# Eighteen of layer 0's thirty-two later modulation pieces computed during the key and query projections

## The chip, the cores and the metric

The kernel runs on one core of a Trainium2 chip. The metric is the device time of one execution in microseconds (us). The engines are TensorE (PE, matmuls; PEld is its weight loading), VectorE (DVE), ScalarE (ACT), GpSimd (POOL) and SyncE (SP), which here only issues DMAs. Each engine works through its own list of instructions; semaphores join the lists.

## The reference

Two layers of a diffusion backbone over 1024 latent tokens and 256 context tokens, model width 1024, all in float32. What this case touches is the beginning of layer 0:

```
silu_c = silu(c); silu_cc = silu(c_ctx)
mod_l = silu_c @ mod_w[0] + mod_b[0];  mod_c = silu_cc @ mod_w[0] + mod_b[0]
sh1, sc1, g1, sh2, sc2, g2 = split(mod_l, 6)          # and the same six of mod_c
h = modulate(rms_norm(x, norm1_g[0]), sh1, sc1)       # latent; context alike
b_g, c_g, xv, q, k, v = split(h @ w_in)
q = rms_norm(q, q_g); k = rms_norm(k, k_g)            # per head of 64; latent ones rotated too
y_conv = b_g * dwconv3(c_g * xv)
o = differential attention(q, k, v)
x = x + g1 * (concat(y_conv, o) @ w_out)
x = x + g2 * conv_ffn(modulate(rms_norm(x, norm2_g[0]), sh2, sc2))
```

`sh1` and `sc1` are needed before anything else. The other four vectors, `g1`, `sh2`, `sc2`, `g2`, for latent and context, are first read after the output projection. They are 4096 rows of `mod_w[0]`, that is 32 pieces of 128, each multiplied with two vectors.

## The kernel before, in words

Every float32 matrix product is three products of split numbers (high and low part of each factor, line 219 to 221), and 24 matmuls of 512 columns make one output tile. A weight unit of 128x1024 is loaded by SP (`wr`, line 107), its high part is cast by ACT (`wh`, line 113), its low part subtracted by DVE (`wl`, line 115). There are two `wr` buffers and five of `wh` and `wl`.

Layer 0's front runs in these stages, and `ev_in` calls them in turn:

- the first modulation vectors and the norms (`mod_start`, `norm`);
- `ev_qkv`: three projections, v, k and q, each over ten tiles of 128 tokens: two context tiles, then eight latent ones. Here the tiles of the keys are called K1 to K10, those of the queries Q1 to Q10. For v a tile is only copied and stored. For k and q each tile goes through `qk_post`: ACT squares it (`qsq`, line 528), DVE sums by head (`ss`, 530) and scales (`vv`, 359), GpSimd raises it to the power -1/2 (`rr`, 361), DVE multiplies (`qn`, 533) and rotates in four operations (`m1`, `m2`, lines 427 to 433; a context tile has a single multiplication `qr`, 537). Then `to_rows` has PE transpose the tile (`tpq`, 545), ACT copy it (`to`, 548) and SP store it. The transposes of a tile are put off: they stand behind the gemm of the tile two places later (`late`).
- the gates: `weave` mixes three generators by their shares: `ev_gates` (36 steps; gemms `pc`, `px`, `pb` and the short convolution), `mod_rest0` (32 steps) and `att_ctx` (the context's attention, 30 steps).

`mod_rest0` makes the 32 pieces. A piece is one 512 KB load on SP into one of two `mbw` buffers (line 312) and two DVE instructions with an accumulator (`mbj`, line 298), one for the latent vector, one for the context's. When all are done it adds the bias and makes two scales.

The order in which an engine's instructions stand is not that of the calls alone: the recording layer moves instructions of one engine past each other while they wait for others, by its own estimate of when they will be ready. On the chip each engine then keeps that order.

Of the kernel before, what the change touches and what calls it, by code (L numbers as in the profile page):

```python
# [54 lines left out]


MODA, MODT, MODR = 128, 3, 5


MOD0 = "TVGVTVTGTVGTVTVT"  # L60
# [13 lines left out]
def drain(gen):  # L74
    for _ in gen:
        pass


def pace(gen, i, n, total):

    for _ in range((i + 1) * total // n - i * total // n):
        next(gen, None)


def weave(*gens):

    live = [[g, n, 0] for g, n in gens]
    while live:
        e = min(live, key=lambda e: (e[2] + 0.5) / e[1])
        if next(e[0], StopIteration) is StopIteration:  # L90
            live.remove(e)
        e[2] += 1
# [46 lines left out]
class Net:  # L139
# [305 lines left out]
    def ev_in(self):  # L445
        nc, tc, I = self.nc, self.tc, self.I
        with ExitStack() as s0:
            hp = s0.enter_context(tc.tile_pool(name="hp", bufs=16, reuse_waits="tile"))
            self.bgp = s0.enter_context(tc.tile_pool(name="bgp", bufs=1, reuse_waits="tile"))
            ps = s0.enter_context(tc.tile_pool(name="psA", bufs=2, space=PSUM, reuse_waits="tile"))  # L450
            alloc = lambda: hp.tile([P, 2, 512], F32R, tag="h", name="h")
            allocc = lambda: hp.tile([P, 2, CTX], F32R, tag="hc", name="hc", bufs=8)
            hs = {c: [] for c in range(3)}
            chunks = ((2, 256, 1), (0, 512, 0), (1, 512, 0))
            with tc.tile_pool(name="xp", bufs=4, reuse_waits="tile") as xp:
                tl, nm = {}, {}

                def load(c, T):
                    src = I["ctxT"] if c == 2 else I["xT"][c]
                    tl[c] = []  # L460
                    for q in range(4):
                        t = xp.tile([P, 2, 512], F32, tag="xr", name="xr", bufs=8)
                        nc.sync.dma_start(t[:, :, :T], src[:, q * 2:(q + 1) * 2, :])
                        tl[c].append(t)

                xtmp = Pool(xp, {"t2k": ("t2k", 6)})
                self.mod_start(hp, ps, lambda: load(2, 256))
                self.ws.ahead = 1
                self.ws.prefetch()
                for c, T, v in chunks:  # L470
                    if c != 2:
                        load(c, T)
                    nm[c] = self.norm(lambda k, c=c, T=T: tl[c][k // 2][:, k % 2, :T], T, self.gs[(0, 1, v)],
                                      lambda k, v=v: self.modA[:, k, v:v + 1], allocc if c == 2 else alloc,
                                      xtmp, ps, hs[c], True)
                    if c == 2:
                        next(nm[2])
                for c, n in ((0, 2), (1, 0), (1, 1)):
                    if n != c:
                        next(nm[c])  # L480
                    drain(nm[n])
                self.ws.ahead = 2
            self.bgw = s0.enter_context(tc.tile_pool(name="bgw", bufs=1, reuse_waits="tile"))
            with tc.tile_pool(name="qkp", bufs=1, reuse_waits="tile") as qp:
                self.ev_qkv(qp, ps, hs)
            with tc.tile_pool(name="gp", bufs=1, reuse_waits="tile") as gp:
                weave((self.ev_gates(gp, ps, hs), 36), (self.mod_rest0(), 32), (self.att_ctx(gp, ps), 30))

    def ev_qkv(self, qp, ps, hs):
        nc, I = self.nc, self.I  # L490
        cosF, sinS = self.rope_tabs(qp)
        qkg = qp.tile([P, 4, 64], F32, name="qkg")
        nc.scalar.dma_start(qkg, I["qkg"])

        nc.vector.tensor_scalar(qkg[:, 0:2, :], qkg[:, 0:2, :], 0.125, None, op0=ALU.mult)
        tabs = {}
        for n, i in (("q", 0), ("k", 2)):
            A = qp.tile([P, 8, 64], F32, name=f"A{n}")
            B = qp.tile([P, 8, 64], F32, name=f"B{n}")
            nc.vector.tensor_tensor(A, cosF, qkg[:, i:i + 1, :].broadcast_to([P, 8, 64]), op=ALU.mult)  # L500
            nc.vector.tensor_tensor(B, sinS, qkg[:, i + 1:i + 2, :].broadcast_to([P, 8, 64]), op=ALU.mult)
            tabs[n] = (A, B)
        tmp = Pool(qp, {"t2k": ("t2k", 7), "qr": ("qr", 4)})
        late = []
        for proj in ("v", "k", "q"):
            W = [self.ws.get() for _ in range(4)]
            for tt in (8, 9, 0, 1, 2, 3, 4, 5, 6, 7):
                c, o = (2, (tt - 8) * P) if tt >= 8 else (tt // 4, (tt % 4) * P)
                pt = ps.tile([P, 512], F32, tag="mm", name="pt", bufs=5)
                self.gemm_tok(pt, W, hs[c], o)  # L510
                if len(late) > 1 or (late and proj == "v"):
                    late.pop(0)()
                if proj == "v":
                    vt = tmp.tile([P, 512], F32, tag="t2k", name="vt")
                    nc.scalar.copy(vt, pt)
                    nc.sync.dma_start(self.vD[tt * P:(tt + 1) * P, :], vt)
                else:
                    qr = self.qk_post(pt, tabs[proj], qkg[:, 0 if proj == "q" else 2, :], tt, tmp)
                    dst = self.qT if proj == "q" else self.kT
                    late.append(lambda qr=qr, dst=dst, tt=tt: self.to_rows(qr, dst, tt, tmp, ps))  # L520
        while late:
            late.pop(0)()
# [1135 lines left out]
```

## Time and profile before

| | us |
|---|---|
| median of 3 runs (2699.24 to 2708.37) | 2703.9 |
| the profiled execution | 2705.93 |
| its span, first to last instruction | 2704.1 |
| PE busy in the span | 2564.4 (95%) |
| DVE busy | 1971.4 (73%) |
| ACT busy | 1164.4 (43%) |
| POOL busy | 425.7 (16%) |

In the trace the keys are projected from about 111 to 174 us, the queries to about 239 us, the gates to 428 us. Busy time is the union of an engine's instructions; matmuls overlap in the pipeline. A wait is the idle time of an engine just ahead of an instruction, put down to what released it.

### The profile page before, as it was taken

What the parts mean: (1) busy time and instruction counts of PE and PEld (TensorE: products, weight loads), DVE (VectorE), ACT (ScalarE), POOL (GpSimd) and SP (SyncE); (2) the same over time, 40 slices, a digit from 0 to 9 for tenths busy, and PEclk for the clock granted to TensorE, in tenths of its full rate; (3) what the DMA queues carried; (4) which work ended last, traced back from release to release, by engine and by line L of the source; (5) the groups of instructions that cost most, each with busy time, mean ns of one, the idle gap of its engine ahead of it and who ended that gap; (6) DMA issues with size and microseconds to landing.
All of it is one profiled execution on the core that took longest, in us unless ns stands there. A gap on an engine that the chain in (4) does not pass through costs nothing.

```text
span 2704.1 us, 34748 instructions
## 1 busy us (share of the span) xinstructions
PE 2564.4 (95%) x12666; PEld 2153.4 (80%) x12666; DVE 1971.4 (73%) x3010; ACT 1164.4 (43%) x1749; POOL 425.7 (16%) x434
## 2 busy tenths in 40 slices
PE   7999998999998898999999998999999999999999
PEld 6877787888898787788887887777678788888887
DVE  7467865999898578877776977626658866666895
ACT  5322223666666454444444444233235444434342
POOL 3222112544432013000000001012203100000000
PEclk9999998999999999999999999999999999999999
DMA  6234535433333542434348665577662322225874
GB/s 253 92 98 140 181 122 159 132 119 121 106 98 102 201 138 86 146 123 133 127 132 301 225 220 171 163 203 224 202 232 81 102 85 86 78 87 174 288 235 158
DMA packets 209548, 414.01 MB, mean 153 GB/s; under 512 B 20320, under 2 KB 89568, under 8 KB 208992
## 3 DMA queue, kind: packets, MB, share of 16 engines
q1 hardware_dynamic: 206352, 406.41, 45.7%
q10 hardware_dynamic: 3024, 5.38, 0.6%
q8 instruction: 99, 1.62, 0.2%
q14 instruction: 73, 0.60, 0.1%
HBM read 341.98 MB, written 69.73 MB: 152 GB/s over the span
## 4 chain that ended last, share of the span: by engine, by line
PE 51%; DVE 14%; issue 12%; DMA 7%; ACT 2%; POOL 2%; SPq 0%; ACTq 0%; DVEq 0%; POOLq 0%
PE PA L219 4%; PE PA L220 4%; PE PA L221 4%; PE pd L220 3%; PE pd L221 3%; PE pd L219 3%; PE PB L220 2%; PE PB L221 2%; PE PB L219 2%; PE po L220 2%; PE po L221 2%; PE po L219 2%; DVE wl L115 2%; DMA mw<-in_mod1T 1%; DMA r<-in_w_up 1%
## 5 line engine op out<-in xcount | busy, mean ns | idle before, releaser
L113 ACT CAST wh<-wr 128x1024 fp32r<-128x1024 f32 x254 | 262.0, 1033 | 411.5 <-PE PA L220 69.6
L115 DVE TENSOR_TENSOR wl<-wr,wh 128x1024 fp32r<-128x1024 f32 (+1 forms) x217 | 273.4, 1262 | 165.0 <-ACT wh L113 162.7
L219 PE MATMUL pd<-s,wh 128*128 128x512 f32 x616 | 240.8, 391 | 4.9 <-ACT s L967 4.9
L220 PE MATMUL pd<-s,wh 128*128 128x512 f32 x616 | 241.1, 391 | 2.0 <-DVE s L968 2.0
L221 PE MATMUL pd<-s,wl 128*128 128x512 f32 x616 | 240.6, 391 | 0.0
L219 PE MATMUL PA<-s,wh 128*128 128x512 f32 x544 | 212.1, 390 | 3.6 <-DVE a L897 3.6
L221 PE MATMUL PA<-s,wl 128*128 128x512 f32 x544 | 211.7, 389 | 0.0
L220 PE MATMUL PA<-s,wh 128*128 128x512 f32 x544 | 211.6, 389 | 0.0
L353 DVE SCALAR_TENSOR_TENSOR mw<-mw,cr 128x256 f32<-128x256 f32 x256 | 111.9, 459 | 82.6 <-DMA mw<-in_mod1T 73.6
L113 ACT CAST wh<-r 128x1024 fp32r<-128x1024 f32 x80 | 67.0, 837 | 219.2 <-PE PB L220 125.2
L361 POOL TENSOR_TENSOR rr<-vv,mhalf 128x8 f32<-128x8 f32 (+2 forms) x39 | 57.6, 1478 | 554.9 <-DVE vv L359 545.8
L219 PEld LDWEIGHTS pd<-s,wh 128*128 128x128 f32 x616 | 116.0, 188 | 29.7 <-ACT s L967 5.8
L220 PEld LDWEIGHTS pd<-s,wh 128*128 128x128 f32 x616 | 116.2, 189 | 27.7 <-DVE s L968 3.6
L221 PEld LDWEIGHTS pd<-s,wl 128*128 128x128 f32 x616 | 116.2, 189 | 24.2
L1480 ACT ACTIVATE p<-S,s 128x1280 f32<-128x1280 f32 (+1 forms) x80 | 92.8, 1160 | 81.3 <-DVE s L1478 73.0
L219 PE MATMUL PB<-s,wh 128*128 128x512 f32 x320 | 124.6, 389 | 1.2 <-ACT p L893 1.2
L220 PE MATMUL PB<-s,wh 128*128 128x512 f32 x320 | 124.5, 389 | 0.0
L221 PE MATMUL PB<-s,wl 128*128 128x512 f32 x320 | 124.5, 389 | 0.0
L219 PEld LDWEIGHTS PA<-s,wh 128*128 128x128 f32 x544 | 102.1, 188 | 26.5 <-DVE a L897 5.3
L822 POOL MEMSET a<- 128x1 f32 x44 | 4.3, 98 | 737.1 <-DVE fcv L707 734.4
L221 PEld LDWEIGHTS PA<-s,wl 128*128 128x128 f32 x544 | 102.1, 188 | 21.2
L220 PEld LDWEIGHTS PA<-s,wh 128*128 128x128 f32 x544 | 102.1, 188 | 21.0
(388 smaller groups left out, 7355.2 us busy)
## 6 DMA issues: line engine op xcount, KB each, us to landing
wr<-in_w_up SPq DMA_DIRECT2D x98, 512.0 KB, 3.4
wr<-in_w_dn SPq DMA_DIRECT2D x92, 512.0 KB, 4.2
gr<-gD SPq DMA_DIRECT2D x154, 256.0 KB, 4.1
mw<-in_mod1T SPq DMA_DIRECT2D x256, 128.0 KB, 3.3
gD<-fcv SPq DMA_DIRECT2D x44, 512.0 KB, 3.6
wr<-in_w_out SPq DMA_DIRECT2D x40, 512.0 KB, 4.2
r<-in_w_up SPq DMA_DIRECT2D x40, 512.0 KB, 3.3
mbw<-in_mod0T SPq DMA_DIRECT2D x32, 512.0 KB, 3.8
```

Source lines behind the costliest of these rows:

```text
L113: self.nc.scalar.copy(hi, raw)
L115: eng.tensor_tensor(lo, raw, hi.bitcast(F32), op=ALU.subtract)
L219: mm(out, L[0], R[0], start=first, stop=False)
L220: mm(out, L[0], R[1], start=False, stop=False)
L221: self.last_mm = mm(out, L[1], R[0], start=False, stop=last)
L353: self.nc.vector.scalar_tensor_tensor(w, in0=w, scalar=1.0, in1=c, op0=ALU.mult, op1=ALU.mult, accum_out=d)
L361: self.last_pow = nc.gpsimd.tensor_tensor(r, vv, self.mhalf[:, :n], op=ALU.pow)
L822: self.nc.gpsimd.memset(a[:, 0:1], 0.0)
L1480: nc.scalar.activation(e, sv, AF.Exp, bias=s2[:, m:m + 1], accum_out=self.s1[:, qt:qt + 1] if m == 0 else s2[:, 2:3])
```

## The change

`mod_rest0` is created ahead of `ev_qkv` and handed to it. From the eleventh tile on, that is for the twenty tiles of k and q, `ev_qkv` takes pieces from the generator behind each tile's gemm, 16 over the 20 tiles. The `weave` of the gates goes on with the same generator at 16 steps in place of 32.

```
+MOD1 = 16
...
             with tc.tile_pool(name="qkp", bufs=1, reuse_waits="tile") as qp:
-                self.ev_qkv(qp, ps, hs)
+                mod = self.mod_rest0()
+                self.ev_qkv(qp, ps, hs, mod)
             with tc.tile_pool(name="gp", bufs=1, reuse_waits="tile") as gp:
-                weave((self.ev_gates(gp, ps, hs), 36), (self.mod_rest0(), 32), (self.att_ctx(gp, ps), 30))
+                weave((self.ev_gates(gp, ps, hs), 36), (mod, 32 - MOD1), (self.att_ctx(gp, ps), 30))
...
-        late = []
+        late, n = [], 0
...
                 self.gemm_tok(pt, W, hs[c], o)
+                n += 1
+                if n > 10:
+                    pace(mod, n - 11, 20, MOD1)
                 if len(late) > 1 or (late and proj == "v"):
```

`pace(gen, i, n, total)` takes the i-th share of `total` steps over n calls. Lines behind the diff's places are three to seven higher in the kernel after (`mbj` is line 301, `qn` 540).

On DVE, the first latent tiles of the keys. Before, tile K3 and the start of K4 (the names are those of the program, `Ak` and `Bk` the rotation tables):

```order
L530 TENSOR_REDUCE ss<-qsq 128x8
L359 TENSOR_SCALAR vv<-ss 128x8
L533 TENSOR_TENSOR qn<-pt,rr 128x512
L427 TENSOR_TENSOR m_1031<-qn,Ak 128x512
L431 TENSOR_TENSOR m_1033<-qn,Bk 128x16x16 x2
L433 TENSOR_TENSOR m_1031<-m_1031,m_1033 128x512
L530 TENSOR_REDUCE ss<-qsq 128x8
```

After, the same tile:

```order
L537 TENSOR_REDUCE ss<-qsq 128x8
L301 SCALAR_TENSOR_TENSOR mbj,modB<-mbw,crow 128x1024
L362 TENSOR_SCALAR vv<-ss 128x8
L301 SCALAR_TENSOR_TENSOR mbj,modB<-mbw,crow 128x1024
L540 TENSOR_TENSOR qn<-pt,rr 128x512
L301 SCALAR_TENSOR_TENSOR mbj,modB<-mbw,crow 128x1024
L430 TENSOR_TENSOR m_1043<-qn,Ak 128x512
L434 TENSOR_TENSOR m_1045<-qn,Bk 128x16x16 x2
L301 SCALAR_TENSOR_TENSOR mbj,modB<-mbw,crow 128x1024
L436 TENSOR_TENSOR m_1043<-m_1043,m_1045 128x512
L537 TENSOR_REDUCE ss<-qsq 128x8
```

Four `mbj` stand inside K3's chain, one of them between `vv` and `qn`, where GpSimd works. By tile there are now 3 (K1), 3 (K2), 4 (K3), 4 (K4) and 2 (K5), 16 in all; before there were none.

On DVE, a latent tile of the queries. Before, tile Q4 (`Aq`, `Bq` are the queries' tables):

```order
L530 TENSOR_REDUCE ss<-qsq 128x8
L359 TENSOR_SCALAR vv<-ss 128x8
L533 TENSOR_TENSOR qn<-pt,rr 128x512
L427 TENSOR_TENSOR m_1586<-qn,Aq 128x512
L431 TENSOR_TENSOR m_1588<-qn,Bq 128x16x16 x2
L433 TENSOR_TENSOR m_1586<-m_1586,m_1588 128x512
```

After, the same tile:

```order
L537 TENSOR_REDUCE ss<-qsq 128x8
L301 SCALAR_TENSOR_TENSOR mbj,modB<-mbw,crow 128x1024
L362 TENSOR_SCALAR vv<-ss 128x8
L301 SCALAR_TENSOR_TENSOR mbj,modB<-mbw,crow 128x1024
L540 TENSOR_TENSOR qn<-pt,rr 128x512
L301 SCALAR_TENSOR_TENSOR mbj,modB<-mbw,crow 128x1024
L430 TENSOR_TENSOR m_1652<-qn,Aq 128x512
L434 TENSOR_TENSOR m_1654<-qn,Bq 128x16x16 x2
L301 SCALAR_TENSOR_TENSOR mbj,modB<-mbw,crow 128x1024
L436 TENSOR_TENSOR m_1652<-m_1652,m_1654 128x512
```

By tile of the queries there are now 3 (Q1), 4 (Q2), 3 (Q3), 4 (Q4), 4 (Q5) and 2 (Q6), 20 in all; before there were six, in Q1 to Q3, one of them between `vv` and `qn`. So 36 of the 64 `mbj`, 18 pieces, stand in the two projections, and 28 in the gates (58 before).

## Rows read from the trace of the kernel before

**Rows 1.** Windows: stretch, length, busy us (x instructions) by engine, granted clock, DMA.
```profile
111.00:174.00 63.00, 62.84 (x293) 51.66 (x291) 35.07 (x64) 15.64 (x24) 15.24 (x10) 1.00 0.26 80
174.00:239.00 65.00, 59.12 (x279) 48.85 (x280) 43.42 (x80) 14.03 (x23) 16.75 (x10) 0.97 0.31 99
239.00:378.00 139.00, 131.28 (x693) 109.92 (x692) 123.01 (x234) 36.77 (x80) 19.87 (x32) 0.99 0.58 188
378.00:428.00 50.00, 49.89 (x263) 42.28 (x261) 12.97 (x24) 8.78 (x16) 3.30 (x6) 1.00 0.24 79
```
**Rows 2.** Waits of DVE, 111 to 239 us: total us, times, longest.
```profile
DVE qn L533 <- POOL rr L361: 33.9, 19, 1.8
DVE ss L530 <- ACT qsq L528: 6.0, 9, 2.3
DVE mbj L298 <- DMA mbw<-in_mod0T: 2.3, 1, 2.3
```
**Rows 3.** DVE's timeline, tiles K2, K3, K6, K7: start, us, instruction [idle before].
```profile
123.17 0.69 DVE L530 TENSOR_REDUCE ss<-qsq 128x8 f32<-128x512 f32 x1 [0.55 <-ACT qsq L528]
129.53 0.69 DVE L530 TENSOR_REDUCE ss<-qsq 128x8 f32<-128x512 f32 x1 [2.30 <-ACT qsq L528]
...
147.27 0.69 DVE L530 TENSOR_REDUCE ss<-qsq 128x8 f32<-128x512 f32 x1 [0.38 <-ACT qsq L528]
148.00 0.17 DVE L359 TENSOR_SCALAR vv<-ss 128x8 f32<-128x8 f32 x1
149.98 0.69 DVE L533 TENSOR_TENSOR qn<-pt,rr 128x512 f32<-128x512 f32 x1 [1.81 <-POOL rr L361]
...
153.19 0.69 DVE L530 TENSOR_REDUCE ss<-qsq 128x8 f32<-128x512 f32 x1 [0.32 <-ACT qsq L528]
```
**Rows 4.** The same view, tiles Q1 to Q5.
```profile
180.90 0.69 DVE L530 TENSOR_REDUCE ss<-qsq 128x8 f32<-128x512 f32 x1 [0.90 <-ACT qsq L528]
...
189.05 1.22 DVE L298 SCALAR_TENSOR_TENSOR mbj<-mbw,crow 128x1024 f32<-128x1024 f32 x1
190.19 0.17 DVE L359 TENSOR_SCALAR vv<-ss 128x8 f32<-128x8 f32 x1
190.31 1.22 DVE L298 SCALAR_TENSOR_TENSOR mbj<-mbw,crow 128x1024 f32<-128x1024 f32 x1
193.06 0.69 DVE L533 TENSOR_TENSOR qn<-pt,rr 128x512 f32<-128x512 f32 x1 [1.52 <-POOL rr L361]
...
203.09 0.68 DVE L530 TENSOR_REDUCE ss<-qsq 128x8 f32<-128x512 f32 x1
...
208.59 0.68 DVE L530 TENSOR_REDUCE ss<-qsq 128x8 f32<-128x512 f32 x1
```
**Rows 5.** GpSimd's timeline: the power of K6 and of Q2.
```profile
148.31 1.64 POOL L361 TENSOR_TENSOR rr<-vv,mhalf 128x8 f32<-128x8 f32 x1 [4.34 <-DVE vv L359]
190.51 2.53 POOL L361 TENSOR_TENSOR rr<-vv,mhalf 128x8 f32<-128x8 f32 x1 [6.93 <-DVE vv L359]
```
**Rows 6.** PE's timeline: the transposes of K6 and of Q3.
```profile
157.30 0.60 PE L545 MATMUL tpq<-ident,m 128*128 128x128 f32 x4
203.58 0.60 PE L545 MATMUL tpq<-ident,m 128*128 128x128 f32 x4
```
**Rows 7.** Waits of PE, 174 to 239 us.
```profile
PE tpq L545 <- DVE m L433: 3.3, 1, 3.3
PE pt L220 <- DVE wl L115: 2.5, 1, 2.5
```
**Rows 8.** Waits of PE, 239 to 378 us (the two largest of six).
```profile
PE tpp L1510 <- DVE p L1493: 2.4, 5, 1.0
PE orb L377 <- POOL r L1533: 1.6, 1, 1.6
```
**Rows 9.** Tile mbw: its loads, and who waited for them.
```profile
  DVE mbj L298: 11.2, 8
...
DMA to landing us min/median/max: 3.2/3.8/7.4
```

More of the change, by code (lines that the diff above doesn't have):

```diff
@@ L484, in ev_in, with ev_qkv @@
             with tc.tile_pool(name="qkp", bufs=1, reuse_waits="tile") as qp:
-                self.ev_qkv(qp, ps, hs)
+                mod = self.mod_rest0()
+                self.ev_qkv(qp, ps, hs, mod)
             with tc.tile_pool(name="gp", bufs=1, reuse_waits="tile") as gp:
-                weave((self.ev_gates(gp, ps, hs), 36), (self.mod_rest0(), 32), (self.att_ctx(gp, ps), 30))
-    def ev_qkv(self, qp, ps, hs):
+                weave((self.ev_gates(gp, ps, hs), 36), (mod, 32 - MOD1), (self.att_ctx(gp, ps), 30))
+    def ev_qkv(self, qp, ps, hs, mod):
         nc, I = self.nc, self.I
```

## The prediction

> **What bounds the kernel now.** I read the busy time by stage first [rows 1]. While the keys are projected (111 to 174 us) PE is busy for 62.8 of 63 us and DVE for 35.1. While the queries are (174 to 239 us) PE is busy for 59.1 of 65, DVE for 43.4. In the first part of the gates (239 to 378 us) DVE is busy for 123.0 of 139 us and PE leaves 139 - 131.3 = 7.7 us idle; in the rest PE is busy throughout. So PE sets the pace nearly everywhere, and where it stops in the gates it is mostly DVE that is late: five waits for `p`, which DVE combines, and one for `r`, a power that hangs on DVE's `e` [rows 8]. By shares, DVE has 27.9 us free beside the keys and 21.6 us beside the queries.
>
> The next view is what DVE waits for in those two stages, since free time counts only if a moved instruction fits into it. Of the idle time 33.9 us are 19 waits of `qn` for GpSimd's power, 6.0 us are 9 waits of `ss` for ACT's square [rows 2]. DVE's list is in order, and the chain of one tile is serial: `ss`, `vv`, power, `qn`, rotation. In K6 `ss` starts at 147.27 and the next one at 153.19, of which only 0.32 us is a wait for the new tile; 1.81 us is the wait for the power in the middle [rows 3]. So DVE's chain for one tile takes 5.6 us of the 5.9 us that PE needs for one, although DVE is idle for more than a third of it.
>
> The third view is how much delay PE tolerates. K6's last rotation is over at about 152.9 us (the next `ss` starts after a 0.32 us wait at 153.19), and PE transposes K6 at 157.30 [rows 3, 6]: 4.4 us of slack. In the queries it is nearly gone: Q3's chain ends when the next `ss` starts, at 203.09, and its transpose is at 203.58 [rows 4, 6]. From there DVE starts each `ss` right behind the last rotation, 5.50 us apart (203.09 to 208.59) with no wait in front. The six `mbj` that already stand in Q1 to Q3 have done that. At the end of the queries PE stops for 3.3 us for a rotated tile, at their beginning for 2.5 us for a `wl` [rows 7]: at both ends DVE's queue decides.
>
> **What the change removes.** Thirty of the 58 `mbj` leave the gates. At 1.22 us each [rows 4] this is 36.6 us of DVE's 123.0 us there, so its share falls from 88% to 62%. The gain is bounded by PE's idle time, 7.7 us [rows 1], and by zero, since the matmuls stay. Not all of it can go: `p` and `qa` also wait for loads, ACT and GpSimd, and a stall that goes leaves the next of these last. I take 4.5 us, a little over half, because the waits named in rows 8 alone are 4.0 us and hang on DVE.
>
> **What it adds in the keys.** First the price of one `mbj` inside a chain. From its start at 189.05 to `vv` at 190.19 it holds the queue for 1.14 us, call it 1.15; between two `mbj` the accumulator's read makes it 1.26. Between `vv` and `qn` one would expect it to be free, for there DVE waits 1.8 us anyway. The trace shows it once, in Q2: `vv` at 190.19, `mbj`, `qn` at 193.06, which is 2.87 us, where K6 without one has 148.00 to 149.98, 1.98 us. The power itself took 2.53 us in place of 1.64 [rows 3 to 5]. So there it costs 0.89 us.
>
> The Trainium skill explains why (SBUF — State Buffer, Who interferes with whom): a DVE instruction with two inputs in SBUF takes its second through the read interface that GpSimd shares, and blocks a GpSimd instruction that reads. The trace agrees in kind; by the page's full block the power would lose the whole 1.22 us, which would put 6 x 0.33 = 2.0 us more into the sum below.
>
> In K1 to K5 there are 16 `mbj`. K1: 1.26 + 1.26 + 1.15 = 3.7. K2: 3 x 1.15 = 3.45. K3 and K4: 3 x 1.15 + 0.89 = 4.34 each. K5: 1.15 + 0.89 = 2.04. Together 17.9 us. What absorbs them is DVE's wait for ACT's squares: 6.0 us in nine waits [rows 2], less the 0.90 us of Q1 [rows 4], which comes after the weights and stays, so 5.1 us. DVE reaches the end of the keys 17.9 - 5.1 = 12.8 us late. PE's 4.4 us of slack is no help in the end: the split of the queries' weights (`wl`) stands in the same queue between the chains of K9 and K10, PE already waits for it without slack [rows 7], and so PE too is 12.8 us late when the queries begin. In between it stops at the transposes of K3, K4 and K5, where the lag passes 4.4 us (about 8, 12 and 14 us).
>
> **What it adds in the queries.** Twenty `mbj` in place of six, 14 more. Between `vv` and `qn` there are now three (Q4, Q5, Q6) in place of one, so the addition is 12 x 1.15 + 2 x 0.89 = 15.6 us. One wait goes: the first `mbj` of the queries waited 2.3 us for its load [rows 2], which now starts ahead of time, as the buffers have long been free. Nothing else absorbs it, for DVE has no wait in front of `ss` from Q4 on [rows 4]. So +13.3 us, 26.1 us in all. At the last transposes PE has the 3.3 us wait already [rows 7]; six short matmuls of the gates now stand ahead of that transpose. A tile's 24 matmuls of 512 columns take at most its 5.9 us [rows 3], 0.25 us each, so six of 256 columns some 0.7 us, which is given back. The gates begin about 25.4 us late.
>
> **Other edits.** The 18 loads stand in SP's queue between the weights and the stores of keys and queries. A load waits for its buffer, so the stores behind it wait for DVE. The first reader of a stored tile is the context's attention in the gates; ten or more us of delay there cost nothing. The fourth unit of the queries' weights stood behind seven stores before and stands behind seven now. Where four `mbj` fall on one tile of 9.8 us, a buffer is empty for about 5 us between two uses, and a load lands in 3.8 us at the median, 7.4 at worst; before, eight waits made 11.2 us over all 64 uses [rows 9]. I take nothing here, and put 3 us to the upper end. PE's clock: the queries, with the 2.5 and 3.3 us waits, show a mean granted clock of 0.97 (1.00 is 2.4 GHz), the keys without a wait 1.00 [rows 1]; in K3 to K5 and Q3 to Q6 a slower PE hides behind DVE's 7 to 10 us a tile, so no price.
>
> **The sum.** 25.4 - 4.5 = +20.9 us. It is a difference within the profiled execution (2705.93 us, span 2704.1), 2 us above the median of 2703.9, so I put it on the median: 2725. If GpSimd's power is not stretched (6 x 0.89 = 5.3 less) and the gates lose all 7.7 us of waits, it is +12.4 (2716). With the full block (2.0), no gain in the gates (4.5) and late loads (3) it is +30.4 (2734).
>
> **Rivals.**
> - Free time takes it all: faster. By shares the 30 added `mbj`, 36.6 us, fit into 27.9 + 21.6 = 49.5 us [rows 1]. Then only the gates change, by 4.5 to 7.7 us: about 2698. Against it: two thirds of that time is the power's wait [rows 2], only six of the 36 stand there, and six were enough to leave Q3 with 0.5 us. It decides if DVE's lag in the keys stays under 4.4 us and the weights' `wl` are not moved.
> - The lag is made and given back: no change. K6 to K10 and Q7 to Q10 have no `mbj`, and PE's tile is 0.3 to 0.4 us longer than DVE's, so a lag shrinks by that on each. If moreover the power's wait hides what stands in it and the gates give the full 7.7 us, and the weights are split ahead of DVE's lag, which would save about 5 more (PE's slack of 4.4 kept), +12.4 becomes about +7: 2711 or less. Against it: the order puts `wl` behind the chain of K9.
> - The gates give nothing: slower still. DVE's waits there may be replaced by others, of ACT and the loads: 25.4 us and no return, 2729; with late loads 2732.
> - That the move doesn't happen is excluded by the order of instructions; it moves 18 pieces, two more than the 16 of the name.
>
> **How the numbers follow.** Forecast 0.65, gates give nothing 0.17, given back 0.10, free time 0.08. This kernel's runs spread over 9 us, and about 0.3%, 8 us, can be told from no change. Faster: the first rival, 0.08. Same: the second, 0.10. Slower: the rest, 0.82. The forecast's own range is 2716 to 2731. For 8 in 10 the range goes from 2708 to 2733: below it lie the faster rival and the lower half of the second, above it a little of the third.
>
> **What would show it.** Right: K3's `ss` to K4's `ss` takes nearly 10 us and PE waits at three transposes of the keys, together 8 to 10 us; the power takes about 2.5 us in the six tiles where an `mbj` stands beside it and 1.64 elsewhere; the first gate matmul is 20 to 27 us later; the queries show waits of PE for `m` at Q3 to Q5; in the gates PE's waits for `p`, `qa` and `r` shrink. Wrong: PE without new waits in the keys, or a lag that is gone before the weights are split, or a gate stage shortened by more than 8 us.

## The result, and the profile after

The kernel after takes 2720.7 us at the median (2711.9 to 2725.9), the one before 2704.1 on the same chip: a ratio of 1.006, 95% interval 1.0044 to 1.0076. That is 16.6 us more; the forecast was 20.9 us more, 2725 us. The profiled execution of after took 2720.46 us, its span is 2718.7 us, 14.6 us more than before's 2704.1.

First the table by stage of after, which answers to [rows 1]; the stretches are the same work, moved by the lag.

```profile
111.00:187.00 76.00, 66.65 (x297) 53.47 (x295) 53.43 (x97) 15.84 (x25) 19.23 (x10) 0.98 0.40 128
187.00:263.00 76.00, 61.79 (x288) 50.42 (x289) 60.01 (x110) 15.02 (x25) 18.65 (x10) 0.95 0.45 145
263.00:395.00 132.00, 129.49 (x678) 108.84 (x678) 85.62 (x170) 35.41 (x79) 14.77 (x32) 0.98 0.39 127
395.00:445.00 50.00, 49.88 (x263) 42.50 (x262) 13.81 (x26) 8.84 (x17) 3.30 (x6) 1.00 0.24 79
```

Keys and queries take 76 us each, where they took 63 and 65. DVE, the third pair of numbers, is busy for 53.4 and 60.0 us: there is still free time, 23 and 16 us of it, while PE idles for 9 and 14 us. Neither engine is full, which is the mark of a chain. What DVE waits for in these two stages, against [rows 2]:

```profile
DVE qn L540 <- POOL rr L364: 32.3, 19, 1.8
DVE wl L118 <- ACT wh L116: 4.5, 2, 3.0
```

The 6.0 us of waits for the squares and the 2.3 us for a load are gone. The wait for the power is almost as long as before (32.3 us against 33.9), although 36 `mbj` were put around it. Where they stand is seen in DVE's timeline of after, tile K3 (start, us, instruction, idle before), against [rows 3]:

```profile
133.65 0.68 DVE L537 TENSOR_REDUCE ss<-qsq 128x8 f32<-128x512 f32 x1
134.25 1.22 DVE L301 SCALAR_TENSOR_TENSOR mbj<-mbw,crow 128x1024 f32<-128x1024 f32 x1
...
135.39 0.17 DVE L362 TENSOR_SCALAR vv<-ss 128x8 f32<-128x8 f32 x1
135.51 1.22 DVE L301 SCALAR_TENSOR_TENSOR mbj<-mbw,crow 128x1024 f32<-128x1024 f32 x1
...
138.26 0.69 DVE L540 TENSOR_TENSOR qn<-pt,rr 128x512 f32<-128x512 f32 x1 [1.52 <-POOL rr L364]
138.87 1.21 DVE L301 SCALAR_TENSOR_TENSOR mbj<-mbw,crow 128x1024 f32<-128x1024 f32 x1
...
140.01 0.69 DVE L430 TENSOR_TENSOR m<-qn,Ak 128x512 f32<-128x512 f32 x1
140.61 0.76 DVE L434 TENSOR_TENSOR m<-qn,Bk 128x256 f32<-128x256 f32 x2
141.28 1.22 DVE L301 SCALAR_TENSOR_TENSOR mbj<-mbw,crow 128x1024 f32<-128x1024 f32 x1
...
142.42 0.69 DVE L436 TENSOR_TENSOR m<-m,m 128x512 f32<-128x512 f32 x1
143.03 0.68 DVE L537 TENSOR_REDUCE ss<-qsq 128x8 f32<-128x512 f32 x1
```

And K7, a tile without an `mbj`, in the same view of after:

```profile
165.32 0.68 DVE L537 TENSOR_REDUCE ss<-qsq 128x8 f32<-128x512 f32 x1
166.04 0.17 DVE L362 TENSOR_SCALAR vv<-ss 128x8 f32<-128x8 f32 x1
168.02 0.69 DVE L540 TENSOR_TENSOR qn<-pt,rr 128x512 f32<-128x512 f32 x1 [1.81 <-POOL rr L364]
168.82 0.69 DVE L430 TENSOR_TENSOR m<-qn,Ak 128x512 f32<-128x512 f32 x1
...
170.83 0.68 DVE L537 TENSOR_REDUCE ss<-qsq 128x8 f32<-128x512 f32 x1
```

K3 takes 143.03 - 133.65 = 9.38 us, K7 5.51. No wait stands in front of either tile's `ss`: DVE goes from chain to chain. Comparing the two tiles step by step gives the price of each of K3's four `mbj`: from `ss` to `vv` 1.74 in place of 0.72, from `vv` to `qn` 2.87 in place of 1.98, from `qn` to the first `m` 1.75 in place of 0.80, and from there to the next `ss` 3.02 in place of 2.01. That is 1.02 + 0.89 + 0.95 + 1.01 = 3.87, the whole difference of the two tiles. GpSimd's powers of K2 and K3 in after, against [rows 5]; K3's, with an `mbj` begun 0.12 us ahead of it, takes 2.59 us in place of 1.64:

```profile
128.48 1.64 POOL L364 TENSOR_TENSOR rr<-vv,mhalf 128x8 f32<-128x8 f32 x1 [7.03 <-DVE vv L362]
135.63 2.59 POOL L364 TENSOR_TENSOR rr<-vv,mhalf 128x8 f32<-128x8 f32 x1 [5.51 <-DVE vv L362]
```

PE's waits of after, first of keys and queries (111 to 262 us, against [rows 7]), then of the gates (262 to 400 us, against [rows 8]):

```profile
PE tpq L552 <- DVE m L436: 18.9, 8, 4.3
PE pt L223 <- DVE wl L118: 4.1, 3, 2.6
PE pt L222 <- ACT wh L116: 0.6, 1, 0.6
```

```profile
PE S L1483 <- DVE qa L1465: 1.7, 1, 1.7
PE pv L223 <- DVE ptl L1519: 0.4, 1, 0.4
PE S L1483 <- ACT p L1487: 0.2, 1, 0.2
```

PE waits for rotated tiles eight times where it waited once. In the gates it waits 2.3 us where it was 7.6 (the 2.4 and 1.6 of [rows 8], and 1.6, 1.2, 0.5 and 0.3 for the other four). The lag can be followed by the start of the same instruction in both traces:

| place | before | after | later by |
|---|---|---|---|
| `ss` of K6 | 147.27 | 159.82 | 12.6 |
| `ss` of K10 | 172.47 | 183.78 | 11.3 |
| PE after its last wait for `wl` of the queries' weights | 177.04 | 188.35 | 11.3 |
| PE's transposes of Q9 | 238.27 | 260.78 | 22.5 |
| first `po` of the output projection | 429.41 | 447.36 | 18.0 |
| end of the span | 2704.1 | 2718.7 | 14.6 |

The rows of PE behind the third and the fourth line, before, then after:

```profile
177.04 0.50 PE L220 MATMUL pt<-wl,hc 128*128 128x512 f32 x1 [2.50 <-DVE wl L115]
238.27 0.63 PE L545 MATMUL tpq<-ident,m 128*128 128x128 f32 x4 [3.34 <-DVE m L433]
```

```profile
188.35 0.50 PE L223 MATMUL pt<-wl,hc 128*128 128x512 f32 x1 [2.57 <-DVE wl L118]
260.78 1.09 PE L552 MATMUL tpq<-ident,m 128*128 128x128 f32 x4 [4.33 <-DVE m L436]
```

### The profile page after: what moved, and what is told of

The parts are those of the page before. It is cut to its first block, busy times and chain, and to the rows that moved or that the text cites. A ratio compares the mean times of both kernels' runs of the same rounds, so it can differ in the third digit from the quotient of the medians.

```text
span 2718.7 us, 34726 instructions
## 1 busy us (share of the span) xinstructions
PE 2568.2 (94%) x12666; PEld 2154.8 (79%) x12666; DVE 1969.4 (72%) x3010; ACT 1164.5 (43%) x1749; POOL 427.1 (16%) x434
## 4 chain that ended last, share of the span: by engine, by line
PE 57%; DVE 17%; issue 12%; DMA 7%; ACT 3%; POOL 3%; SPq 0%; ACTq 0%; DVEq 0%; POOLq 0%
PE PA L222 4%; PE PA L223 4%; PE PA L224 4%; PE pd L223 3%; PE pd L222 3%; PE pd L224 3%; PE PB L222 2%; PE PB L223 2%; PE PB L224 2%; DVE wl L118 2%; PE po L223 2%; PE po L224 2%; PE po L222 2%; POOL rr L364 2%; DVE mbj L301 2%
## 5 line engine op out<-in xcount | busy, mean ns | idle before, releaser
L364 POOL TENSOR_TENSOR rr<-vv,mhalf 128x8 f32<-128x8 f32 (+2 forms) x39 | 64.0, 1640 | 570.6 <-DVE vv L362 568.3
```

The lines of the kernel that those rows point to most:

```text
L364: self.last_pow = nc.gpsimd.tensor_tensor(r, vv, self.mhalf[:, :n], op=ALU.pow)
```

## The experiments

Theory A was that DVE's in-order list costs the time: a tile's chain is serial, so an `mbj` between its steps adds itself to the chain although DVE waits in it. Kernels of one group ran together with the kernel before, whose median moved from 2705.9 to 2709.1 us between the groups; so the ratios count.

**The loads alone.** The moved pieces are loaded as in after; DVE reads two columns of each in place of the two products, so these 18 pieces are left out of the result.

```
+            if mt < 18:
+                nc.vector.tensor_copy(self.modB[:, mt, :], w[:, 0:2])
+            else:
+                self.matvec(w, 2, ...)
```

> The kernel after, but the first 18 pieces are only loaded: in place of the two mbj of a piece DVE copies two columns of the loaded tile, so these 18 pieces of the modulation vectors are left out. The loads, their queue and their buffers stay. Theory A (what costs is DVE's time in its in-order list, about 1 us per mbj): the keys run as before (K3's ss to K4's ss near 5.9 us), no new wait of PE at the transposes, the gates keep their gain of about 4.5 us and the wait of 3.3 us at the last transposes goes too: 2697 us (2693 to 2702). Rival B (the 18 loads on SP's queue and in the DMA engines cost the time, by weights or stores that come late): it stays near 2715 to 2721.

2700.8 us, ratio 0.9975 (0.9964 to 0.9985), 5 us faster than before by the medians, 7 by the ratio, as A forecast. DVE's small reads did wait for their loads:

```profile
DVE modB L317 <- DMA mbw<-in_mod0T: 12.0, 6, 3.2
```

But K10's `ss` is at 175.44, only 3.0 us late (K1's was already 1.7 late, at 120.21), the transposes of Q9 at 240.22 (+2.0), and the first `po` at 425.84, 3.6 us early. So the loads, with their queue, are not what costs 16.6 us: rival B falls.

**Half as many pieces.** `MOD1 = 8`. By the order this gives 8 `mbj` in the keys and 12 in the queries (the expectation counted 7 and 11).

> The kernel after with 8 pieces in place of 16 for the projections. Theory A with a wait that absorbs: K1 to K3 get 7 mbj, about 7 us, of which DVE's waits for the squares absorb 5.1, so the keys end 2 us late; the queries get 11 in place of 6, 5 us more, less the 2.3 us wait for the first load: 3 us. The gates have about 12 mbj fewer and give back about 2: in all +3 us, 2707 (2703 to 2711), that is less than a fifth of the whole change for half of it. Rival C (each moved mbj costs the same, nothing absorbs): half of 16.6, 2712.

2709.0 us, ratio 1.0015 (1.0002 to 1.0027): 3 to 4 us more than before. Half the dose costs a quarter of the whole (0.0015 against 0.006), near A; the interval runs from almost nothing to 45% of the whole, just short of C's half. The trace of one execution says a third to two fifths: K10's `ss` is 3.7 us late in place of 11.3, the transposes of Q9 8.7 in place of 22.5, the first `po` 5.9 in place of 18.0. At each place it is less than half, as the first `mbj` go into DVE's waits for the squares.

**Six pieces beside the v projection,** none called beside keys and queries.

```
-                if n > 10:
-                    pace(mod, n - 11, 20, MOD1)
+                if 4 < n <= 10:
+                    pace(mod, n - 5, 6, MOD1)          # MOD1 = 6
```

> The kernel after, but the pieces taken early stand beside the v projection (six pieces, tiles 5 to 10 of it) and none is called beside keys and queries; the other 26 come in the gates. DVE is idle there from 91.1 to 108.5 us. Theory A: twelve mbj, 14 us, fit in front of the first wl of the keys' weights, keys and queries run as before, the gates have 12 mbj fewer: 2702 us (2698 to 2705). Rival B (loads in SP's queue between the v stores delay the keys' weights): the first ss of the keys comes 3 us or more later and the time is 2707 or more.

2706.5 us, ratio 1.0004 (0.9992 to 1.0015): no difference. The interval, from 2 us less to 4 us more, reaches from A's 2702, 2 us below before, to beyond rival B's 2707, so the time doesn't decide. DVE's timeline shows where six pieces end:

```profile
109.57 1.23 DVE L301 SCALAR_TENSOR_TENSOR mbj<-mbw,crow 128x1024 f32<-128x1024 f32 x1 [1.03 <-DMA mbw<-in_mod0T]
...
111.98 2.35 DVE L118 TENSOR_TENSOR wl<-wr,wh 128x1024 fp32r<-128x1024 f32 x2
```

The keys' first `wl` starts at 111.98, where it started at 108.55. Of these 3.4 us, 1.3 lay ahead of it, for ACT begins the cast `wh` at 108.73 in place of 107.47; it ends at 109.78, and the other 2.2 are DVE's: twelve `mbj` with 6.9 us of waits for loads between them are longer than the 17.4 us that stood free. Rival B's sign is there (K1's `ss` is 3.8 us late), but not its cause: the next load of the keys' weights starts at 113.23, right behind the first `wl`, which frees its buffer, as before (109.81, with that `wl` from 108.55 to 109.78). Again it is DVE's list, but filled by waits for loads, which my sum of 14 us had left out. K10's `ss` is 5.1 us late; by the first `po`, 1.4 us late, the gates have given most of it back.

**The chain cut in two.** The pieces stay where after has them. On DVE, `ss` and `vv` of a tile now come ahead of `qn` and the rotation of the tile before.

```
-                    qr = self.qk_post(pt, tabs[proj], ...)
-                    late.append(lambda ...: self.to_rows(qr, ...))
+                    a = self.qk_first(pt, tmp)             # square, ss, vv, power
+                    if half:
+                        half.pop(0)()                      # qn, rotation of the tile before
+                    half.append(second)                    # this tile's, and its to_rows to late
...
+        with self.tc.issue_after(self.last_vv.ins):
             nc.vector.tensor_tensor(g3(qn), g3(pt), ...)
```

> The kernel after, with the chain of a tile cut in two on DVE: the ss and vv of a tile stand ahead of the qn and the rotation of the tile before, so the power runs while DVE rotates; the transposes of a tile come one tile later. The moved pieces stay (16 called, all mbj of K1 to K5 and Q1 to Q7 as before). Theory A (the cost comes from the serial chain with the power's wait of 1.8 us inside): a tile without mbj takes DVE about 3.7 us in place of 5.5, an mbj 1.2, so the keys' list is 54 us of 63; no lag at the weights of the queries, no wait for qn: 2697 us (2692 to 2704). Rival D (an mbj costs about 1 us whatever stands around it, as the SBUF or GpSimd is slowed): 2715 or more.

2690.4 us, ratio 0.9945 (0.9929 to 0.9961): 15 us faster than before, and 2 us below A's range. Windows of keys and queries, then DVE's timeline of a whole step:

```profile
111.00:174.00 63.00, 63.00 (x293) 52.13 (x292) 51.88 (x96) 16.30 (x24) 16.36 (x10) 1.00 0.47 149
174.00:239.00 65.00, 64.89 (x323) 53.92 (x322) 63.22 (x120) 16.57 (x28) 16.36 (x10) 1.00 0.57 183
```

```profile
136.31 0.68 DVE L544 TENSOR_REDUCE ss<-qsq 128x8 f32<-128x512 f32 x1
137.02 1.23 DVE L301 SCALAR_TENSOR_TENSOR mbj<-mbw,crow 128x1024 f32<-128x1024 f32 x1
...
138.17 0.17 DVE L546 TENSOR_SCALAR vv<-ss 128x8 f32<-128x8 f32 x1
138.25 0.68 DVE L558 TENSOR_TENSOR qn<-pt,rr 128x512 f32<-128x512 f32 x1
138.85 1.21 DVE L301 SCALAR_TENSOR_TENSOR mbj<-mbw,crow 128x1024 f32<-128x1024 f32 x1
...
143.01 0.68 DVE L544 TENSOR_REDUCE ss<-qsq 128x8 f32<-128x512 f32 x1
```

`qn` follows `vv` at once, as its power was computed in the step before. The step with three `mbj` takes 6.70 us, and in the queries DVE is busy for 63.2 of 65 us while PE is busy for 64.9: the free time that after could not use is used. In the two stages PE waits for no rotated tile and no `wl`, and DVE not once for a power (32.3 us in after). The edit also puts each transpose about one PE tile later (K1's at 132.80 in place of 127.73); this alone could not hide after's lag of 11.3 and 22.5 us. Rival D falls.

**The control: the cut chain, no piece moved** (the same edit on the kernel before).

> The kernel before with the cut chain of the previous experiment and no piece moved: the control. Theory A (the chain was late at both ends of the queries): PE's waits for the last rotated tiles and for wl, 3.3 and 2.5 us, go, since the six mbj of Q1 to Q3 no longer lengthen the chain; the gates keep their 58 mbj and their 7 to 8 us of waits: 2699 us (2696 to 2703), so that the moved pieces are worth about 8 us of the 15 that the interleaved kernel with pieces gained. Rival E (all of that gain is the interleaving, the pieces are neutral): 2690.

2697.7 us, ratio 0.9968 (0.9955 to 0.9982), some 9 us faster than before, within A's range; its profiled execution was the longest of its nine (span 2703.1). The waits at both ends of the queries are gone, those of the gates have stayed:

```profile
PE tpp L1528 <- DVE p L1511: 2.7, 5, 1.1
PE orb L377 <- POOL r L1551: 2.2, 1, 2.2
```

So the same moved pieces are worth about -6 us on the cut chain (15 less 9) and +16.6 us on the serial one. The two ratios' intervals overlap a little, so the 6 us may be as good as none, or 12. The traces agree on the sign: from 239 to 378 us PE waits 3.0 us in all with the pieces moved and 9.8 without, and the first `po` stands at 414.33 and 425.27 (429.41 in the kernel before). Rival E falls: its 2690 is a ratio of 0.9948, outside the control's interval.

**Twenty-four pieces on the cut chain.** `MOD1 = 24`, 25 `mbj` in the keys and 25 in the queries.

> The interleaved kernel with 24 pieces called beside keys and queries in place of 16: 25 mbj in the keys and 25 in the queries by the order. Theory A (DVE's list is free until it is full): the keys' list would be 35.1 + 25 x 1.22 = 65.6 us of 63, the queries' about 36 + 30.5 = 66.6 of 65, so DVE gets about 2 to 4 us late at the weights of the queries and at their end, and the gates have almost no wait left to lose: 2693 us (2690 to 2698), slower than with 16. Rival F (time goes down with every piece that leaves the gates): 2688 or less.

2697.8 us, ratio 0.9966 (0.9955 to 0.9976): some 6 us slower than with 16 by the ratios, whose intervals overlap a little, and as A says. DVE's list in the queries is full, and PE waits for rotated tiles again; with 16 it did not. PE's wait, and the queries' window:

```profile
PE tpq L570 <- DVE m L436: 1.8, 4, 0.6
```

```profile
174.00:239.00 65.00, 64.42 (x315) 53.31 (x314) 64.10 (x123) 16.91 (x27) 17.79 (x11) 1.00 0.61 191
```

The first gate matmul comes at 231.69, with 16 pieces at 227.80, and the first `po` at 419.95 and 414.33. The waits are 1.8 us of these 5.6; K1's transposes came 1.5 us later already, and the rest stays open. (The transposes of Q9, at 246.85 and 234.79, don't measure a lag: with 24 pieces more of the gates' matmuls stand ahead of them.)

**Twelve pieces, and sixteen with three more beside v,** both on the cut chain.

> The interleaved kernel with 12 pieces: 12 mbj in the keys and 16 in the queries, 36 in the gates. Theory A: no wait in the projections as with 16; the gates keep a little more of their waits (8 mbj more): 2691 us (2689 to 2695).

> The interleaved kernel with 16 pieces beside keys and queries and 3 more beside the v projection (6 mbj, which by the earlier run with six pieces fit between 91 and 103 us, ahead of the keys' first wl): 24 mbj stay in the gates. Theory A: the keys start as with 16, the gates have 2 to 3 us of waits left and lose little of it: 2689 us (2686 to 2692). If the three loads delay the keys' weights, as six did, 2692 or more.

2694.6 us, ratio 0.9954 (0.994 to 0.9968), and 2692.6 us, ratio 0.9947 (0.9931 to 0.9963). On before's 2704.1 these ratios are 2691.7 and 2689.8, within A's two ranges. Neither can be told from 16 pieces (0.9945), so no gain of three more pieces beside v is seen, and the optimum is flat from 12 to 16. The lowest ratio is that of the cut chain with 16.

**The pieces spread evenly,** on the serial chain.

```
+            with self.tc.issue_after(self.hold.ins) if self.hold else nullcontext():
                 self.matvec(w, 2, ...)                      # hold: the last ss
```

> The kernel after with its 16 pieces spread: the two mbj of a piece may not stand ahead of the ss of the tile before, so 16 tiles of keys and queries have two mbj each, one between ss and vv and one between vv and qn (16 in the keys, 16 in the queries), in place of three or four on some tiles and none on the last ones. Theory A (in the serial chain every mbj adds its time, wherever it stands): a tile with two takes 5.50 + 1.02 + 0.89 = 7.4 us on DVE in place of PE's 5.9, eight of them in the keys make 15.3 us, less the 4 to 5 us that DVE's waits for the squares absorb: the keys end 10 to 11 us late, the queries 7 to 9 more, the gates give back 4 and what follows some 2: 2718 us (2713 to 2722). Rival G (the lumps of three and four mbj on a tile are what makes PE wait; spread, they fit the free time): 2708 or less.

2713.9 us, ratio 1.0017 (1.0005 to 1.0029): +4.6 us, with an interval from 1.4 to 7.8. That is 2709 on before's 2704.1: A's time, 2713 at least, is missed, and rival G's 2708 lies inside the interval. The traces show A's mechanism all the same: the price per tile is as forecast, and PE waits 12.7 us for rotated tiles, in eight waits, so the spread pieces don't fit the free time either. DVE's timeline, tile K4:

```profile
139.06 0.68 DVE L539 TENSOR_REDUCE ss<-qsq 128x8 f32<-128x512 f32 x1
139.66 1.22 DVE L301 SCALAR_TENSOR_TENSOR mbj<-mbw,crow 128x1024 f32<-128x1024 f32 x1
...
140.92 1.23 DVE L301 SCALAR_TENSOR_TENSOR mbj<-mbw,crow 128x1024 f32<-128x1024 f32 x1
...
143.67 0.69 DVE L542 TENSOR_TENSOR qn<-pt,rr 128x512 f32<-128x512 f32 x1 [1.52 <-POOL rr L366]
...
146.40 0.68 DVE L539 TENSOR_REDUCE ss<-qsq 128x8 f32<-128x512 f32 x1
```

From `ss` to `ss` this is 7.34 us, forecast 7.4. PE goes on after its last `wl` at 184.77, 7.7 us later than before (forecast 10 to 11: three of the four `wl` now stand in K9's chain, two before); the transposes of Q9 are 17.0 us late, so the queries added 9.3 (7 to 9). The first `po` is 10.0 us late: the gates gave back 7.0 (forecast 4). In its profiled execution the end is 8.9 us late. So A had two sizes wrong, PE's lag behind the keys and what the gates give back, and spreading is better than lumps by more than the four `mbj` that it holds fewer (5.5 us already at the transposes of Q9). What share the order of the `wl` and the gates' own order have in it, these runs don't separate.

## Why the prediction was right, and where it was off

The direction, the mechanism and the place were right. The forecast's terms against the trace:

| term | forecast | measured |
|---|---|---|
| keys, to the weights of the queries | +12.8 | +11.3 |
| queries, to the transposes of Q9 | +13.3 | +11.2 |
| gates, with the six short matmuls ahead of them | -4.5 - 0.7 = -5.2 | -4.5 (22.5 to 18.0) |
| behind the gates | 0 | -3.4 (18.0 to 14.6) |
| sum, in the profiled executions | +20.9 | +14.6 |

- **The price of an `mbj` was mis-sized: 1.15 us forecast, 1.0 measured.** I had taken the time from its start to the next instruction's. But between dependent instructions DVE has, in these rows, a gap of its own, which an independent `mbj` fills: `ss` of 0.68 us, then `vv` 0.72 behind its start; with an `mbj` in between that starts after 0.60. The price is the difference of two tiles, not the length of a row. In the keys the 16 `mbj` come, by the starts of `ss` tile by tile and the waits that they took the place of, to 3.6 + 3.1 + 3.9 + 3.9 + 1.9 = 16.4 in place of 17.9 (K1's three in a row are the dearest, 1.2 each); less the 5.1 of absorbed waits this is 11.3, as measured (K1 began 0.3 late, and K6 to K8 took 0.3 less together). In the queries the starts of `ss` from Q1 to Q9 are 12.2 us further apart than before: 14.5 for the 14 added `mbj`, forecast 15.6, less the 2.3 us of the wait for the load.
- **Beside the power an `mbj` costs 0.89 us,** as forecast from a single row: 2.87 - 1.98 in K3, with a power of 2.59 in place of 1.64. That the power's wait would hide it, a part of the rivals, is out, and so is the full 1.22 us.
- **The absorption of 5.1 us** held, and half the dose cost less than half. But all 6.0 us of waits for squares are gone, also Q1's 0.90, which the prediction let stay. Before, PE's granted clock averaged 0.66 from 177 to 182 us, behind its wait for `wl`; after, it was 1.00 from 188.3 to 192 us. K9's transposes took 1.05 us before and 0.60 after, and Q1's square stands behind their copy on ACT. So Q1's `ss` is 10.5 us late and not 11.3. With this 0.8, and 0.2 for the place of the `wl` in Q9, the 12.2 become the 11.2 of the table.
- **PE's slack of 4.4 us was no help,** as forecast: PE is as late behind its last `wl` (11.3) as DVE at K10. In the keys it stops at two transposes, K3 and K4, not three, for 2.8 and 3.3 us, 6.1 together in place of 8 to 10, as each `mbj` was cheaper.
- **The check on `ss`** held: 9.38 us from K3 to K4 ("nearly 10"). The first gate matmul is at 254.31 in place of 233.5, 20.8 us later (20 to 27 forecast).
- **The gates** gave back what was forecast, in part by luck. The six short matmuls are seen: 16 stand ahead of Q9's transposes in place of 10, 0.12 us apart. Their 0.7 us is part of the 4.5, so that 3.8 us are left of the forecast 4.5, though PE's waits fall by 5.3, from 7.6 to 2.3 us.
- **Behind the gates** the forecast had nothing, and 3.4 us came back. A part is PE's clock. At the start of the output projection PE has waited in both kernels (1.2 and 1.8 us), and its matmuls start 0.21 us apart; 0.12 apart, at a granted clock of 1.00, they are from 437.32 in the kernel before, 7.9 us behind the first `po`, and from 452.92 in the kernel after, 5.6 us behind. The mean granted clock up to there was 0.57 and 0.70. Why it rose sooner, these runs don't show. The first `st` of the norm that follows is 16.7 us late, so 1.3 us came back here. The other 2.1 us lie further on and stay open; they fall within what separates executions of one kernel, and the medians, 16.6 apart, have them not.

Of the rivals, "free time takes it all" was wrong for this chain, but right for the cut one: the shares of busy time told how much could fit, the order within the list decided whether it did. That is what the first view had left open, and the second, the waits of DVE, had answered.

## What to carry to other kernels

In this kernel the free time of an in-order engine was of use only where it lay between chains. If it lies inside a chain, as a wait for another engine, an instruction put there adds its time; first stagger the chain over two tiles, so that the wait is filled with the other tile's steps, and then move work in. Price a moved instruction by the difference between two tiles, with and without it, not by the length of its row. And count the waits for its loads as part of its time on the engine.

## What the runs showed of the hardware

GpSimd's power on 128x8 takes 1.64 us, and 2.48 to 2.60 us (over all runs) when DVE's 128x1024 product of two SBUF tiles, or a `wl`, has started before it. In the cut chain all 20 powers take 1.64 us, although an `mbj` starts while ten of them run; there `qn`, which reads PSUM, is running when the power starts, and the `mbj` comes behind it:

```profile
138.48 1.64 POOL L548 TENSOR_TENSOR rr<-vv,mhalf 128x8 f32<-128x8 f32 x1 [5.12 <-DVE vv L546]
```

The `mbj` beside this one (138.85, 1.21 us) isn't longer either. The Trainium skill (SBUF — State Buffer, Who interferes with whom) has it that the issue order decides who is blocked, and that a DVE instruction with two SBUF inputs contends with a GpSimd instruction that reads SBUF. The stretched powers agree with both. Where the power has begun first, the `mbj` should then be the one that is blocked, and there the traces differ: beside those ten powers the `mbj` take 1.21 to 1.23 us, their usual length, and the powers 1.64.
